# A two-layer transformer trunk: the compressed branch's inputs laid out token by token, by engines in place of four transfers

## The chip, the cores and the metric

The kernel runs on one core of a Trainium2 chip. The metric is device time in microseconds (us), the median of several runs. Before the change it is 640.43 us (three runs, 640.12 to 640.68).

## The reference, cut to what matters

Two layers of a decoder for 256 tokens of 1024 features, in float32: `x += mixer(norm(x))` and `x += relu(norm(x) @ w1)^2 @ w2` in each, then a last norm. The first layer's mixer joins native sparse attention (compressed, selected and window branches) with differential attention; the second layer's is block attention. The change touches the compressed branch's keys and values only:

```
def compress_kv(kv, pos, w1, w2):                  # keys or values: 2 heads (g) of 64
    nc = (s - CMP_BLOCK) // CMP_STRIDE + 1         # 15 windows of 32 tokens, one every 16
    tok = jnp.arange(nc)[:, None] * CMP_STRIDE + jnp.arange(CMP_BLOCK)[None, :]
    blk = kv[:, :, tok] + pos
    hid = jax.nn.gelu(blk.reshape(b, g, nc, CMP_BLOCK * d) @ w1)      # 2048 -> 128
    return hid @ w2                                                   # 128 -> 64
...
    lc = jnp.einsum('bgrqd,bgcd->bgrqc', qb, kc) * scale + tbl_gr[:, :, t5_bucket(rel_c)]
    pc = masked_softmax(lc, rel_c >= 0)            # the compressed branch
    oc = jnp.einsum('bgrqc,bgcd->bgrqd', pc.astype(vc.dtype), vc)
```

## The kernel before, in words

**Numbers in two parts.** Every matmul operand is split into a high part (a copy to a shorter format, ScalarE) and a low part (the rest, VectorE); a product is three matmuls: high x high, high x low, low x high (`mm3`, L530 to L532). Weights come from HBM in pieces of 128x1024 through five raw buffers (SyncE's queue, `load`, L403) and are split by ScalarE (L470) and VectorE (L473) into one of six pairs of parts.

**The stages.** Layer 0's projections go unit by unit in the order vg, k, q0, c, q1, h, dv, d0 to d3. "c" gives the inputs of the compression, "h" is its first layer (`unit_hid`, L1026). The softmax maps of the window and selected branches begin when their q unit is done; the first two query groups' maps run beside q1, h and dv. Behind h stand `cmp_hidden` (the activation and second layer), `cmp_softmax` (the compressed logits of all heads), and the values. The maps of the other two query groups begin when the first two have given back their two banks of PSUM, which takes the compressed branch's values as well. The differential heads and the output projection follow.

**The first layer of the compression.** `got_ckv` (L926) takes the bank of unit c, 128 rows (two heads of 64 features) by 2 x 256 (keys and values, tokens), writes a high copy (ScalarE, L515) and a low part (VectorE, L521) to a tile `kcv`, and lays both out in `mT[1]` (named mTl in the trace, not yet in use for the mixer's output). There the lower 64 partitions hold the first half of a window's tokens and the upper 64 the second half. The layout is by part, key or value, head, block (15, and a sixteenth that holds the positional terms), and the 16 tokens of a half innermost. Four transfers on SyncE's queue bring `kcv` there, one for each head and half. The first layer then runs 16 steps of two matmuls (L1039 and L1040: weights high and low, 256 columns), each with one token's 128 values (part, key or value, head, block) as the stationary operand, so neighbours of this operand lie 16 elements apart.

**What sets the order.** No engine is scheduled by hand. A planner (`Plan`, L201) runs a rough model of the engines: each step has a duration, an urgency (lower goes first) and the events it waits for, and each engine takes the most urgent step that is ready. The steps are issued in that order, and each engine's queue runs them in that order on the chip. Steps of `got_ckv` have urgency 0; a map's steps 0.001 times its number; units of columns 1; a weight split -1 if its piece is among the next two in use, else 3. A map's scaling (L827) can be done by GpSimd or VectorE, whichever is free first in the model. A bank of PSUM is read by one engine at a time: a step on another engine waits in the model for 0.2 us behind the last reader.

Of the kernel before, what the change touches and what calls it, by code (L numbers as in the profile page):

```python
# [177 lines left out]
def t_dve(n):  # L178
    return 0.0685 + n / 960
# [21 lines left out]
class Plan:  # L201
    """Puts the program's steps out in the order in which a rough model of the engines begins them:
    each engine takes the most urgent step whose inputs are there."""
# [17 lines left out]
    def when(self, deps, line, fn):  # L221
        """Calls fn as soon as the line can see all of deps done."""
        deps = [d for d in deps if d is not None]
        left = [sum(d.time is None for d in deps)]

        def go():
            t = max([self.now] + [d.time + (0.0 if d.line in (line, None) else SEEN) for d in deps])
            self.at(t, fn)

        def one():  # L230
            left[0] -= 1
            if not left[0]:
                go()

        if not left[0]:
            go()
        else:
            for d in deps:
                if d.time is None:
                    d.then.append(one)  # L240

    def step(self, choices, deps=(), urgency=1, bank=None):
        """choices: (line, time, emit) of the engines that can do the step."""
        self.count += 1
        s = Step(urgency, self.count, bank)
        for line, dur, emit in choices:
            self.when(deps, line, lambda line=line, dur=dur, emit=emit: self.arrive(line, s, dur, emit))
        return s.done
# [44 lines left out]
    def spawn(self, gen):  # L293
        """Runs gen; each value it yields is the events it waits for."""
        ev = Event()

        def go():
            try:
                w = next(gen)
            except StopIteration:  # L300
                self.fire(ev)
                return
            w = [w] if isinstance(w, Event) else w
            self.when(w, None, go)

        self.at(self.now, go)
        return ev
# [8 lines left out]
class Slots:  # L316
    """Buffers that are handed on; the one who gets it waits for its last use."""
# [22 lines left out]
    def recall(self, item):  # L340
        """Takes an item out as soon as it is free."""
        ev = Event()
        if any(item is i for i in self.items):
            self.items = [i for i in self.items if i is not item]
            self.plan.fire(ev)
        else:
            self.wanted.append((item, ev))
        return ev
# [14 lines left out]
@with_exitstack  # L363
def trunk_kernel(ctx: ExitStack, tc: tile.TileContext, x, w, prm_d, gs, cst_d, eye, out, widths):
# [32 lines left out]
    def load(dst, src, deps=(), line=SP, u=0, lat=1.3):  # L397
        """A transfer: issued by an engine, then in turn with the others on the queues."""
        eng = {SP: nc.sync, ACT: nc.scalar, POOL: nc.gpsimd}[line]
        n = int(np.prod(dst.shape)) * 4  # L400
        ev = Event()
        dur = {SP: 0.45, ACT: 0.4, POOL: 1.04}[line]
        issued = plan.step([(line, dur, lambda: eng.dma_start(dst, src))], deps, u)  # L403

        def move():
            Plan.moved = max(Plan.moved, plan.now + lat) + n / 0.34e6
            plan.at(Plan.moved + 0.5, lambda: plan.fire(ev))

        plan.when([issued], None, move)
        return ev  # L410
# [4 lines left out]
    def halves(pair):  # L415
        """Room for two pieces in a pair of tiles that are not in use."""
        v = [a.rearrange("p k s -> p (k s)") for a in pair]
        return [(v[0][:, 1024 * i:1024 * i + 1024], v[1][:, 1024 * i:1024 * i + 1024]) for i in range(2)]
# [92 lines left out]
    def split_out(hi, lo, src, n, deps, scale=None, bank=None, u=0):  # L511
        """The high part by ACT, the rest by DVE."""
        def high():
            if scale is None:
                nc.scalar.activation(hi, src, AF.Copy)  # L515
            else:
                nc.scalar.activation(hi, src, AF.Copy, scale=scale)

        def low():
            if scale is None:  # L520
                nc.vector.tensor_tensor(lo, src, hi.bitcast(F32), OP.subtract)  # L521
            else:
                nc.vector.scalar_tensor_tensor(lo, src, scale, hi.bitcast(F32), op0=OP.mult, op1=OP.subtract)  # L523

        e = act(t_act(n), high, *deps, u=u, bank=bank)
        return [e, dve(t_dve(n), low, e, u=u, bank=bank)]
# [7 lines left out]
    def rstd(t, deps):  # L534
        """(mean(x[t]^2) + eps)^-1/2; ACT squares the left columns and DVE the right ones, starting from the left's
        sum where those come first."""
# [22 lines left out]
    def rvar(t, deps):  # L559
        """1 / (mean(x[t]^2) + eps)."""  # L560
# [6 lines left out]
    def to_xT(t, g, xT, xe, rs, deps, back=()):  # L567
        """Steps that write x[t] * g (* rs) transposed into xT."""
# [78 lines left out]
    def unit_N(src, cuts, n, done):  # L647
        """One bank of columns for each row tile."""
# [13 lines left out]
    def units_N(src, dones):  # L662
        """Two banks of columns for each row tile; part of the second comes before the second tile's first."""
# [16 lines left out]
    def row_mm(bank, src, deps, pc, kt, t, n, prev, first, last, u=1):  # L680
        """bank += rows t of src's column tile kt @ half n of the piece's columns."""
# [57 lines left out]
    begun = []  # L739

    def urgency():
        """Earlier maps go first."""
        begun.append(0)
        return 0.001 * len(begun)

    def logits_exp(q, k, par, h, P, sums, b, deps, u):
        """exp(q.k + bias - max) of one map: [q0 x k0 | q1 x k0 k1], and the row sums."""
# [30 lines left out]
    def turned_P(A, deps, u):  # L778
        """The transposed probabilities, in two parts."""
# [24 lines left out]
    def head_map(q, k, par, h, v, v_e, gate, pair, deps, seen=None):  # L804
        """One causal softmax map of a head; its part of the pair's outputs is added to po."""
# [32 lines left out]
    class Pair:  # L838
        """The outputs of two heads, gathered in one bank."""
# [27 lines left out]
    # ================= layer 0: mixer =================  # L867
# [26 lines left out]
    def first_norms():  # L894
        """g over all rows by the tensor engine; it stays in PSUM for the time."""
# [27 lines left out]
    ckv = mT[1].rearrange("p (h k g) (c i) -> p h k g c i", h=2, k=2, c=16)  # L923
    ckv_e = Event()

    def got_ckv(b, evs):  # L926
        """Both parts of the compression's inputs, the second half-block's tokens below the first's."""
        kcv = acts.tile([128, 2, 2, S], F32R, name="kcv", tag="scr")
        ps = b.t.rearrange("p (a t) -> p a t", a=2)
        ev = split_out(kcv[:, 0], kcv[:, 1], ps, 512, evs, bank=b)  # L930
        bank_a.put(b, [ev[1]])
        pos = prm[:, P_POS:P_POS + 32].rearrange("p (k i) -> p k i", k=2)[:, :, None, :].to_broadcast([128, 2, 2, 16])
        done = split_out(ckv[:, 0, :, :, 15, :], ckv[:, 1, :, :, 15, :], pos, 64, [prm_e])
        for g in range(2):
            for s in range(2):
                done.append(load(ckv[64 * s:64 * s + 64, :, :, g, 0:15, :].rearrange("p h k c i -> p (h k) (c i)").bitcast(F32),
                                 kcv[64 * g:64 * g + 64, :, :, 16 * s:16 * s + 240].rearrange("p h k t -> p (h k) t").bitcast(F32),
                                 ev))
        yield done
        plan.fire(ckv_e)  # L940

    def stack_q(dst, ps, b, deps, u=0):
        """Both parts of q / 8 of a head's rows: one in the head's half, the other in the other half."""
# [11 lines left out]
    def stack_k(hi, lo, ps, b, deps, u=0):  # L955
        """The high part of k twice, and the low part over zeros."""
# [69 lines left out]
    def unit_hid():  # L1026
# [5 lines left out]
        for q in range(4):  # L1032
            pc = next_piece()
            for ii in range(4):
                def emit(pc=pc, q=q, ii=ii):
                    pc.use()
                    c = slice(256 * ii, 256 * ii + 256)
                    lhs = ckv[:, :, :, :, :, 4 * q + ii]
# [10 lines left out]
    def cmp_hidden(ba, e):  # L1049
        """Compressed keys and values."""  # L1050
# [51 lines left out]
    def cmp_softmax():  # L1102
        """The compressed branch of the eight heads in one."""
# [176 lines left out]
    def add_to_x(bank, slots, dep, t, n, rs=None):  # L1280
        """x[t] += bank (* rs)."""
# [11 lines left out]
    def out_proj(m_e, x_free, nxt):  # L1293
        """x += m @ w; the first tokens go ahead, and their norm runs beside the products of the others.
        Two of the pieces lie in the room of the transposed x."""
# [38 lines left out]
    def mlp(src, x_ready, nxt):  # L1334
        """x += relu(norm(x) @ w1)^2 @ w2, the norm's factor of each token squared at the end."""
# [21 lines left out]
        def turned(t, b, evs):  # L1357
            """Tokens are the rows here: to be turned."""
# [76 lines left out]
    def next_stage(gi, norm):  # L1435
        """The transposed (normed) x of the next stage, one token tile after the other."""
# [19 lines left out]
    def program():  # L1456
# [19 lines left out]
        # layer 1  # L1476
# [44 lines left out]
    def final(t, evs):  # L1521
# [4 lines left out]
        def job():  # L1526
            """x * g waits for the norm's factor."""
# [40 lines left out]
```

## Time and profile before

| | |
|---|---|
| median of the runs | 640.43 us (640.12 to 640.68) |
| profiled execution, span from its first to its last instruction | 638.6 us (the page gives no other time of it) |
| busy: TensorE, weight loads | 623.5 us, 562.5 us |
| busy: VectorE, ScalarE, GpSimd | 402.3, 358.8, 80.8 us |
| granted clock of TensorE, mean | 0.996 |
| moved by DMA | 110.49 MB, 173 GB/s |

Instructions of TensorE are pipelined, and the profile shows each with its whole length, so their lengths add up to more than the time; what one costs is the distance from its start to the next one's start. Weight loads have a row of their own (PEld) and overlap the matmuls. A wait in the profile is the idle time of an engine ahead of an instruction, put down to what released it last. Names: `ps` is a bank of PSUM, `whi` and `wlo` a weight piece's parts, `xTh` and `xTl` the transposed tokens' parts, `P` a map, `mTl` the tile in which the compression's inputs lie.

### The profile page before, as it was taken

The page shows a single profiled execution, that of the slowest core. Times are in us where ns is not written, and L with a number is a line of the kernel's source. Part 1 is how long each engine was busy: PE and PEld are TensorE (multiplying, and loading weights), DVE is VectorE, ACT ScalarE, POOL GpSimd, SP SyncE. Part 2 cuts the span into 40 slices and gives each one's busy share as a digit, 9 for nine tenths or more (in the row PEclk, how much of TensorE's full clock was granted, in tenths as well). Part 3 has the DMA queues.
Part 4 walks back from the last instruction along what each step waited for, and adds up shares of the span by engine and source line. Part 5 has one row for each costly group of instructions (what it writes and reads, how often), then busy time and mean ns, then how long its engine had stood idle before and what let it go on. Part 6 is the DMA issues. An engine that isn't in the chain of part 4 may idle for free.

```text
span 638.6 us, 10541 instructions
## 1 busy us (share of the span) xinstructions
PE 623.5 (98%) x4022; PEld 562.5 (88%) x4022; DVE 402.3 (63%) x723; ACT 358.8 (56%) x645; POOL 80.8 (13%) x105
## 2 busy tenths in 40 slices
PE   7999999999999999999999999999999999999995
PEld 5999899778899898999988999978889999898994
DVE  6888698869554545445477688785964454544434
ACT  6777488747645445444444588764764444445421
POOL 2022022210201001011120020110020100101011
PEclk8999999999999999999999999999999999999999
DMA  7995432325765565656527433443576555565501
GB/s 280 320 304 190 141 105 96 131 101 185 256 212 191 179 199 165 204 191 214 183 73 236 155 121 111 132 133 120 173 267 202 195 179 193 176 200 176 165 2 66
DMA packets 33188, 110.49 MB, mean 173 GB/s; under 512 B 3425, under 2 KB 6769, under 8 KB 33138
## 3 DMA queue, kind: packets, MB, share of 16 engines
q1 hardware_dynamic: 32274, 107.21, 51.7%
q0 software_dynamic: 576, 2.10, 0.9%
q8 instruction: 31, 0.51, 0.3%
q10 hardware_dynamic: 288, 0.52, 0.2%
q14 instruction: 19, 0.16, 0.1%
HBM read 107.76 MB, written 1.07 MB: 170 GB/s over the span
## 4 chain that ended last, share of the span: by engine, by line
PE 86%; DVE 6%; ACT 4%; issue 2%; DMA 1%; POOL 1%; SPq 0%; POOLq 0%; DVEq 0%; ACTq 0%
PE ps L531 26%; PE ps L530 26%; PE ps L532 26%; PE ps L756 2%; DVE wlo L473 2%; PE ps L790 1%; DVE KZ L964 1%; PE ps L593 1%; DVE QD L951 1%; ACT KD L961 1%; DMA x<-in_x_dram 1%; ACT QD L947 1%; POOL P L827 1%; ACT KD L960 1%; PE ps L1040 1%
## 5 line engine op out<-in xcount | busy, mean ns | idle before, releaser
L473 DVE TENSOR_TENSOR wlo<-raw,whi 128x1024 fp32r<-128x1024 f32 (+1 forms) x157 | 189.3, 1217 | 74.1 <-ACT whi L470 72.6
L470 ACT ACTIVATE whi<-raw 128x1024 fp32r<-128x1024 f32 (+1 forms) x157 | 163.5, 1052 | 96.8 <-PE ps L532 70.3
L530 PE MATMUL ps<-xTh,whi 128*128 128x256 f32 x592 | 168.9, 285 | 0.0
L531 PE MATMUL ps<-xTl,whi 128*128 128x256 f32 x592 | 166.4, 281 | 0.0
L532 PE MATMUL ps<-xTh,wlo 128*128 128x256 f32 x592 | 166.3, 281 | 0.0
L530 PEld LDWEIGHTS ps<-xTh,whi 128*128 128x128 f32 x592 | 111.7, 189 | 1.1 <-ACT gates L996 0.3
L531 PEld LDWEIGHTS ps<-xTl,whi 128*128 128x128 f32 x592 | 111.7, 189 | 0.7
L532 PEld LDWEIGHTS ps<-xTh,wlo 128*128 128x128 f32 x592 | 111.6, 189 | 0.0
L1348 POOL TENSOR_TENSOR P<-P 128x512 f32<-128x512 f32 x32 | 35.8, 1120 | 320.5 <-ACT P L1345 319.0
L473 DVE TENSOR_TENSOR mTl<-raw,mTh 128x1024 fp32r<-128x1024 f32 x34 | 43.2, 1272 | 23.9 <-ACT mTh L470 23.9
L470 ACT ACTIVATE mTh<-raw 128x1024 fp32r<-128x1024 f32 x34 | 36.0, 1059 | 30.2 <-PE ps L531 20.4
L1345 ACT ACTIVATE P<-ps 128x512 f32<-128x512 f32 x32 | 19.0, 595 | 52.2 <-PE ps L532 52.2
L530 PE MATMUL ps<-whi,Th 128*128 128x512 f32 x120 | 46.9, 391 | 0.0
L532 PE MATMUL ps<-whi,Tl 128*128 128x512 f32 x120 | 46.9, 391 | 0.0
L531 PE MATMUL ps<-wlo,Th 128*128 128x512 f32 x120 | 46.9, 390 | 0.0
L1350 DVE TENSOR_TENSOR Tl<-P,Th 128x512 fp32r<-128x512 f32 x22 | 15.2, 693 | 50.1 <-POOL P L1348 50.1
L770 ACT ACTIVATE P<-P,nm 128x128 f32<-128x128 f32 x80 | 35.5, 447 | 13.5 <-DVE nm L766 13.5
L532 PE MATMUL ps<-xTh,mTl 128*128 128x256 f32 (+1 forms) x128 | 38.1, 297 | 0.7 <-DVE mTl L523 0.7
L530 PE MATMUL ps<-xTh,mTh 128*128 128x256 f32 (+1 forms) x128 | 38.7, 302 | 0.0
L531 PE MATMUL ps<-xTl,mTh 128*128 128x256 f32 (+1 forms) x128 | 38.0, 297 | 0.0
L530 PE MATMUL ps<-whi,xTh 128*128 128x512 f32 (+1 forms) x88 | 34.2, 389 | 0.0
L531 PE MATMUL ps<-wlo,xTh 128*128 128x512 f32 (+1 forms) x88 | 33.3, 378 | 0.2 <-DVE wlo L473 0.2
(219 smaller groups left out, 1193.0 us busy)
## 6 DMA issues: line engine op xcount, KB each, us to landing
raw<-in_w_dram SPq DMA_DIRECT2D x192, 512.0 KB, 4.1
B<-ud SPq DMA_DIRECT2D x1, 2048.0 KB, 11.3
gB<-in_gs_dram POOLq DMA_DIRECT2D x4, 512.0 KB, 4.3
x<-in_x_dram SPq DMA_DIRECT2D x2, 512.0 KB, 4.4
mTl<-kcv SPq DMA_DIRECT2D x4, 240.0 KB, 6.8
raw<-in_w_dram SPq DMA_DIRECT2D x2, 420.0 KB, 6.2
out_dram<-P SPq DMA_DIRECT2D x2, 256.0 KB, 2.0
out_dram<-P ACTq DMA_DIRECT2D x2, 256.0 KB, 2.5
```

The costliest lines, as they stand in the source:

```text
L470: nc.scalar.activation(pc.hi[:, :n], raw[:, :n], AF.Copy)
L473: nc.vector.tensor_tensor(pc.lo[:, :n], raw[:, :n], pc.hi[:, :n].bitcast(F32), OP.subtract)
L530: nc.tensor.matmul(out_, ah, bh, start=start, stop=False)
L531: nc.tensor.matmul(out_, ah, bl, start=False, stop=False)
L532: nc.tensor.matmul(out_, al, bh, start=False, stop=stop)
L593: nc.tensor.transpose(p[:, 128 * k:128 * k + 128], xs[:, 128 * k:128 * k + 128], ident)
L756: nc.tensor.matmul(ps[:, 128 * qt:128 * qt + nk], q[:, par, ts], k[i][:, par, :nk], start=i == 0, stop=i == 1)
L770: nc.scalar.activation(P[:, c], P[:, c], AF.Exp, bias=nm[:, qt:qt + 1], scale=-1.0, accum_out=sums[:, qt:qt + 1])
L790: nc.tensor.transpose(pt[:, c], A[:, c], ident)
L1345: e = act(t_act(512), lambda: nc.scalar.activation(r, b.t, AF.Relu), got, *deps)
L1348: g = pool(1.225, lambda: nc.gpsimd.tensor_tensor(sq, r, r, OP.mult), e)
L1350: h = dve(t_dve(512), lambda: nc.vector.tensor_tensor(hl, sq, hh.bitcast(F32), OP.subtract), f, g)
```

## The change: a new layout, and engine copies for the four transfers

The inputs lie by token first and block last: `ckv_rows[:, i]` is the 128 values of token i, side by side, and is the stationary operand of step i. `kcv` holds the high copy alone (one ScalarE copy of the whole bank, 128x512). For each of the four pairs of head `g` and half `s`, the 64 partitions of the head go to the 64 partitions of the half: the high part by GpSimd from `kcv` where both are the same partitions, else by ScalarE from the bank; the low part by VectorE, from the bank and `kcv`. Each of these handles 64 partitions x 480 elements, reads at a distance of 16 elements and writes runs of 15. The positional terms are written at every sixteenth element. The bank goes back when all readers of it are done. The comments of the file are taken out as well.

```diff
-    ckv = mT[1].rearrange("p (h k g) (c i) -> p h k g c i", h=2, k=2, c=16)
+    ckv_rows = mT[1].rearrange("p a b -> p (a b)").rearrange("p (i m) -> p i m", i=16)
+    ckv = ckv_rows.rearrange("p i (h k g c) -> p h k g i c", h=2, k=2, g=2)
...
-        kcv = acts.tile([128, 2, 2, S], F32R, name="kcv", tag="scr")
+        kcv = acts.tile([128, 2, S], F32R, name="kcv", tag="scr")
         ps = b.t.rearrange("p (a t) -> p a t", a=2)
-        ev = split_out(kcv[:, 0], kcv[:, 1], ps, 512, evs, bank=b)
-        bank_a.put(b, [ev[1]])
+        whole = act(t_act(512), lambda: nc.scalar.activation(kcv, ps, AF.Copy), *evs, bank=b)
...
-        done = split_out(ckv[:, 0, :, :, 15, :], ckv[:, 1, :, :, 15, :], pos, 64, [prm_e])
+        done = split_out(ckv[:, 0, :, :, :, 15], ckv[:, 1, :, :, :, 15], pos, 64, [prm_e])
+        out = []
         for g in range(2):
+            r = slice(64 * g, 64 * g + 64)
             for s in range(2):
-                done.append(load(ckv[64 * s:64 * s + 64, :, :, g, 0:15, :].rearrange("p h k c i -> p (h k) (c i)").bitcast(F32),
-                                 kcv[64 * g:64 * g + 64, :, :, 16 * s:16 * s + 240].rearrange("p h k t -> p (h k) t").bitcast(F32),
-                                 ev))
+                o, t = slice(64 * s, 64 * s + 64), slice(16 * s, 16 * s + 240)
+                def part(h, src, r=r, o=o, t=t, g=g):
+                    return ckv[o, h, :, g, :, 0:15], src[r, :, t].rearrange("p k (c i) -> p k i c", i=16)
+                def hi(part=part):
+                    dst, src = part(0, ps)
+                    nc.scalar.activation(dst, src, AF.Copy)
+                def same(part=part):
+                    dst, src = part(0, kcv)
+                    nc.gpsimd.tensor_copy(dst, src.bitcast(F32))
+                def lo(part=part):
+                    (dst, src), (_, high) = part(1, ps), part(1, kcv)
+                    nc.vector.tensor_tensor(dst, src, high.bitcast(F32), OP.subtract)
+                if g == s:
+                    done.append(pool(0.9, same, whole))
+                else:
+                    out.append(act(t_act(480), hi, *evs, bank=b))
+                out.append(dve(t_dve(480), lo, whole, bank=b))
+        bank_a.put(b, [whole, *out])
+        done += out
         yield done
...
-                    lhs = ckv[:, :, :, :, :, 4 * q + ii]
+                    lhs = ckv_rows[:, 4 * q + ii]
```

## Rows read from the trace of the kernel before

**Rows 1.** The page, part 1: busy us (share of the span) and instructions per engine.

```profile
PE 623.5 (98%) x4022; PEld 562.5 (88%) x4022; DVE 402.3 (63%) x723; ACT 358.8 (56%) x645; POOL 80.8 (13%) x105
```

**Rows 2.** The page, part 4: shares of the chain that ended last, by engine.

```profile
PE 86%; DVE 6%; ACT 4%; issue 2%; DMA 1%; POOL 1%; SPq 0%; POOLq 0%; DVEq 0%; ACTq 0%
```

**Rows 3.** Stretches: length, busy us of each engine (instructions), granted clock, DMA share, GB/s.

```profile
37.50:61.40 23.90, 23.90 (x177) 23.77 (x176) 20.76 (x66) 19.43 (x52) 7.24 (x9) 1.00 0.70 214
61.40:73.70 12.30, 12.30 (x70) 10.55 (x69) 6.81 (x14) 3.99 (x7) 0.14 (x2) 1.00 0.40 124
73.70:105.00 31.30, 31.30 (x254) 30.45 (x254) 29.33 (x97) 24.24 (x70) 6.24 (x7) 1.00 0.43 138
105.00:129.00 24.00, 22.32 (x156) 19.69 (x154) 21.18 (x65) 19.36 (x59) 4.88 (x8) 1.00 0.33 117
```

**Rows 4.** Instructions on tile mTl up to 150 us: duration ns min/median/max, first and last start.

```profile
L1039 PEld LDWEIGHTS ps<-whi,mTl x16: 291/316/318, 49.6 to 58.3; 128*128 128x128 f32 x16
...
L403 SPq DMA_DIRECT2D mTl<-kcv x4: 600/692/1673, 40.0 to 42.1; - x4
...
DMA to landing us min/median/max: 6.6/6.8/7.2
```

**Rows 5.** The page, part 5: a projection's weight loads, busy us and mean ns of one.

```profile
L531 PEld LDWEIGHTS ps<-xTl,whi 128*128 128x128 f32 x592 | 111.7, 189 | 0.7
```

**Rows 6.** The chain that ended last from 49.5 to 59 us, by line.

```profile
by line: PE ps L1040 37.6%; PE ps L1039 37.5%; PE ps L790 10.6%; PE ps L530 6.6%; PE ps L532 4.9%; PE ps L531 4.8%; PE ps L756 1.3%
```

**Rows 7.** Timeline of TensorE: start us, length us, engine, line, operation, out<-in.

```profile
36.32 0.28 PE L530 MATMUL ps<-xTh,whi 128*128 128x256 f32 x1
...
39.44 0.28 PE L532 MATMUL ps<-xTh,wlo 128*128 128x256 f32 x1
...
49.61 0.48 PE L1039 MATMUL ps<-whi,mTl 128*128 128x256 f32 x1
```

**Rows 8.** Timeline of SyncE's queue from 40 us.

```profile
40.03 3.79 SPq L403 DMA_DIRECT2D mTl<-kcv  x4
```

**Rows 9.** TensorE's waits (20 to 160 us; then weight loads, whole span): total us, times, longest.

```profile
PE ps L530 <- DVE KZ L964: 1.1, 1, 1.1
...
PEld ps L790 <- POOL P L827: 1.8, 4, 0.7
```

**Rows 10.** Instructions on tile kcv.

```profile
L515 ACT ACTIVATE kcv<-ps x1: 597/597/597, 38.7 to 38.7; 128x512 fp32r<-128x512 f32 x1
L521 DVE TENSOR_TENSOR kcv<-ps,kcv x1: 690/690/690, 39.3 to 39.3; 128x512 fp32r<-128x512 f32 x1
```

**Rows 11.** Groups on ScalarE, then VectorE, 30 to 60 us: busy us, mean ns of one.

```profile
L947 ACT ACTIVATE G<-ps 64x256 fp32r<-64x256 f32 x8 | 3.0, 378 | 0.6 <-PE ps L532 0.5
...
L964 DVE TENSOR_TENSOR KL<-ps,KK 64x256 fp32r<-64x256 f32 x1 | 0.4, 427 | 0.0
```

**Rows 12.** The compressed logits' additions, by source line: duration ns min/median/max.

```profile
L1133 DVE TENSOR_TENSOR cmpb<-ps,B x4: 192/222/254, 73.8 to 74.4; 128x28 f32<-128x28 f32 x2, 128x60 f32<-128x60 f32 x2
...
L1140 DVE TENSOR_TENSOR cmpb<-cmpb,ps x2: 215/247/279, 74.1 to 74.7; 128x56 f32<-128x56 f32 x1, 128x120 f32<-128x120 f32 x1
```

**Rows 13.** Timeline of VectorE: the splits of weights between 34 and 60 us.

```profile
34.67 2.36 DVE L473 TENSOR_TENSOR wlo<-raw,whi 128x1024 fp32r<-128x1024 f32 x2
...
45.73 1.22 DVE L473 TENSOR_TENSOR wlo<-raw,whi 128x1024 fp32r<-128x1024 f32 x1
...
58.31 2.35 DVE L473 TENSOR_TENSOR wlo<-raw,whi 128x1024 fp32r<-128x1024 f32 x2
```

**Rows 14.** Timelines of GpSimd and of the weight loads: the first map's scaling and transposes.

```profile
40.55 0.61 POOL L827 TENSOR_SCALAR P<-P,co,gates 128x256 f32<-128x256 f32 x1 [31.45 <-DVE co L820]
...
42.05 0.35 PEld L790 LDWEIGHTS ps<-ident,P 128*128 128x128 f32 x3
```

**Rows 15.** GpSimd's scalings: by source line, then the longest in the timeline.

```profile
L827 POOL TENSOR_SCALAR P<-P,co,gates x15: 449/626/2746, 40.5 to 99.7; 128x256 f32<-128x256 f32 x14, 128x128 f32<-128x128 f32 x1
...
58.21 2.71 POOL L827 TENSOR_SCALAR P<-P,co,gates 128x256 f32<-128x256 f32 x1 [4.56 <-DVE co L820]
```

## The prediction

> **What bounds the kernel now.** I read the busy table first: TensorE is busy for 98% of the span, VectorE for 63% and ScalarE for 56% [rows 1]. The chain of work that ended last says the same, 86% of the span on TensorE [rows 2]. The whole kernel is then a queue of matmuls, and whatever shortens a matmul pays unless an engine that feeds it is late. So the stage around the change is read by stretches [rows 3]: from 37.5 to 105 us TensorE has no gap, and its granted clock is 1.00, the 2.4 GHz level. VectorE is busy for 20.76 of 23.90 us up to 61.4, for only 6.81 of 12.30 us after it, and for 29.33 of 31.30 us up to 105. Only from 105 to 129 us does TensorE lose time (22.32 of 24.00).
>
> In this stage the 32 matmuls of the compression's first layer stand out. Their weight loads take 316 ns [rows 4], while every projection's load of the same 128x128 takes 189 [rows 5]. They are the instructions that read the compression's inputs with 16 elements between neighbours. From 49.5 to 59 us the chain is theirs for 37.6 + 37.5% of 9.5 us [rows 6], which is 7.13 us, or 0.223 us for each. A projection also streams 256 columns per matmul and starts one every 0.12 us: its 27 starts from 36.32 to 39.44 us span 26 intervals [rows 7]. The moving columns are equal, so I put the difference down to the weight load.
>
> **The change part by part.**
>
> *The layout.* The 128 weights of each matmul now lie side by side, as in a projection. Both operands then have the projection's form, so I take its interval: 32 x (0.223 - 0.120) = 3.30 us less on TensorE, on the path. Bounds: 0 if the distance is not the reason, 3.4 if the interval comes down to 0.117.
>
> *The transfers removed.* Four issues on SyncE took 3.79 us from 40.03 us, and each landed 6.8 us after its issue [rows 4, 8]; the last, issued at 42.1, landed at about 48.9. TensorE came to the first layer at 49.6 and did not wait for them: its longest wait between 20 and 160 us is 1.1 us, for a later stage [rows 7, 9]. Nothing on the path goes with them. The issues and the traffic are worth 0; what is gained is that the inputs can be ready earlier, and no one needs them earlier than 49.6 less what TensorE gains on the way. Bounds: 0 to -0.3.
>
> *ScalarE.* The whole-bank copy stays: before 597 ns for 128x512 [rows 10]. Added are two copies of 64x480. By the nearest rows, 378 ns for 64x256 [rows 11] and 597 for 128x512, one takes about 0.57, 1.1 us together. Their reads step over 16 elements; if that costs what it costs the weight load (316/189 = 1.67), 1.9 us. ScalarE was busy for 19.43 of 23.90 us [rows 3], so it has 4.5 us of room and I cost it at 0.
>
> *VectorE.* One subtraction of 128x512 (690 ns) becomes four of 64x480. By the rows for 64x256 (427 ns) and 128x512 each takes 0.66, together 2.65, so 1.96 us are added. These read both operands at a distance of 16. The bias addition of the compressed logits reads one operand so: from 28 to 60 elements it grows from 192 to 254 ns, 1.94 ns per element, where a packed one grows from 215 to 279 ns between 56 and 120 elements, 1.0 ns [rows 12]. At 1.94 one takes 0.14 + 480 x 0.00194 = 1.07, together 4.3, so 3.6 us are added. I lean to the upper half, some 3 us, since the row with the same distance is the nearer one. In the stretch from 37.5 to 61.4 VectorE had 3.14 us without work, and TensorE now wants to leave this stretch 3.3 us earlier, so up to 3 us of VectorE's work no longer fits. What can move is there: two weight splits (2.35 us) stand at 58.31 [rows 13], for pieces that TensorE comes to only after some 65 us, and the 12.3 us behind 61.4 have 5.5 us of room [rows 3]. So the sum of the work costs 0 on the path; its place does not.
>
> *Its place.* The four subtractions and the copies come at about 39.3 to 44 us, at a higher urgency than the first softmax maps, whose VectorE and GpSimd steps run there. The first map's scaling on GpSimd ran from 40.55 to 41.16 and its transposes on TensorE began at 42.05 [rows 14], so there was 0.9 us to spare. Behind the waiting transpose stands all of TensorE, and nothing else can pass it. The plan that lays out the order counts 0.57 us for a subtraction and 0.9 us for a GpSimd copy, and puts q's columns ahead of the transposes accordingly; only what the operations take beyond that can stall TensorE. For VectorE that is 4 x (1.07 - 0.57) = 2.0 us at the upper price and 0.4 at the lower, less the 0.9 to spare: a stall of 0 to 1.1 us. I take 0.6.
>
> *GpSimd.* Two copies of 64x480 from SBUF. The rows for scaling 256 and 128 elements, 626 ns (the median) and 449 (the shortest, the one with 128) [rows 15], give 1.38 ns per element, so 0.93 us each. The longest of these rows took 2746 ns: it ran from 58.21 while VectorE did two splits [rows 13, 15], whose two inputs both lie in SBUF. Two such copies would end 5.4 us after 39.3 instead of 1.9. No split stood on VectorE between 37.0 and 45.7 [rows 13], so I take 0.93 each, inside the plan's 0.9, and 0 on the path.
>
> The Trainium skill speaks against this part. GPSIMD Engine Reference, section Performance pitfalls for Q7 kernels, says that a read of SBUF with more than 8 bytes between elements costs some half more per element; these copies step 64 bytes. By it a copy would take about 1.3 us, an estimate from that page, and the sum would come to 638.4 if all of the 0.7 us beyond two copies of 0.93 became waiting; no row of this case shows it.
>
> *Small ones.* The positional part is written at single elements instead of runs of 16; 242 and 219 ns at 30 us, far ahead of its use. The bank of the inputs is held some 3 us longer; the next user of that pair comes at 49.6. Both 0.
>
> Sum: -3.30 + 0.6 = -2.7 us. The path behind this stage is TensorE's to 105 us and then follows the last projection through ScalarE and VectorE, so I carry it to the end in full. The profiled execution has a span of 638.6 us, and the median of the three runs is 640.43, so 1.8 us lie around the span, which the change does not touch. 640.43 - 2.7 = 637.7.
>
> **The rivals.**
>
> *A, the engines take it back.* TensorE gains 3.3 us but VectorE, at 94% from 73.7 to 105 us, does not: it would have to start that stretch earlier, and the compressed logits that start it come through a chain of small VectorE steps that stand behind the extra 3 us. For it: the 94%. Against it: VectorE's 5.5 us of room just ahead, and TensorE's lack of waits [rows 9]. If all but 0.5 to 1 us is lost: 639.4 to 640; with the 3 us of VectorE work fully on the path, 640.1.
>
> *B, slower: the first maps starve TensorE.* One mechanism: the two GpSimd copies stand ahead of the first four scalings in GpSimd's queue, and a weight split on VectorE beside them stretches each to 2.7 us. Then the first scaling ends at 39.3 + 5.4 + 0.6 = 45.3 instead of 41.2, and TensorE, which reaches the transposes at 42 us plus what the plan puts ahead of them, stands still for up to 4 us, and for another 0.9 with the subtractions at their upper price. It decides the sign from a stall of 3.3 us on; at 4.9 it gives 642.0. For it: TensorE has already waited for these scalings, 1.8 us in four places of the whole span [rows 9]. Against it: no split stood there.
>
> *C, more than the term.* The inputs are ready earlier, the compressed branch ends earlier, and the maps of the last four query groups start earlier, which fills part of the 1.7 us that TensorE loses after 105: 635.5.
>
> *D, it doesn't do what it says.* The 316 ns are not due to the distance. Then only the stall of 0.6 us is left: 641.0. Against it: no other difference to a projection's load is to be seen.
>
> **How the numbers follow.** Forecast (636.4 to 639.1): 0.60. A: 0.18, of which 0.04 below 639.1, 0.12 within 0.2% and 0.02 above. B: 0.10. C: 0.07. D: 0.05, of which 0.01 is slower. A measurement of this kernel tells about 0.2%, 1.3 us, from no change: faster is below 639.1, slower above 641.7. Faster: 0.60 + 0.07 + 0.04 = 0.71. Same: 0.12 + 0.04 = 0.16. Slower: 0.10 + 0.02 + 0.01 = 0.13. The range from 635.9 to 640.9 leaves out most of C's lower part (0.05) and B with the worst of A and D (0.13).
>
> **What would show it.** Right: weight loads of the first layer at 189 ns, a start every 0.12 us, its 32 matmuls in 3.8 us, four subtractions of 0.66 to 1.07 us, TensorE's waits for scalings near 41 to 46 us below 1 us in sum, the same share of TensorE after 129 us. Wrong: loads that stay at 316 (D); GpSimd copies above 2 us with transposes waiting for scalings (B); a first layer 3.3 us shorter with waits of TensorE for VectorE between 61 and 129 us (A).

## The result, and the profile after

The changed kernel takes 647.36 us (median of four runs, 646.16 to 648.28; the kernel before beside it 640.55). The ratio is 1.0099, interval 1.0085 to 1.0113: it is slower by some 6.3 us, where 2.7 us less were forecast. Below, a difference in us is a run's ratio less one, times 640.5; the intervals of such ratios are 0.1 to 0.25% to either side.

The first layer itself did what was forecast. The rows on tile mTl of the changed kernel (duration in ns, least, median, most; first and last start) answer to [rows 4, 10]:

```profile
L1063 PEld LDWEIGHTS ps<-whi,mTl x16: 187/188/190, 45.6 to 50.6; 128*128 128x128 f32 x16
...
L954 DVE TENSOR_TENSOR mTl<-ps,kcv x4: 992/998/1007, 40.4 to 43.4; 64x480 fp32r<-64x480 f32 x4
...
L946 ACT ACTIVATE mTl<-ps x2: 564/568/571, 39.2 to 39.8; 64x480 fp32r<-64x480 f32 x2
L950 POOL CAST mTl<-kcv x2: 1018/1026/1035, 39.2 to 40.3; 64x480 fp32r<-64x480 f32 x2
```

The timeline of TensorE has 26 matmuls of the layer in a row:

```profile
47.89 0.29 PE L1063 MATMUL ps<-whi,mTl 128*128 128x256 f32 x1
...
50.82 0.28 PE L1064 MATMUL ps<-wlo,mTl 128*128 128x256 f32 x1
```

The loads fell from 316 to 188 ns, and these 25 intervals are 0.117 us each, where 0.223 was before and 0.120 was forecast. The layer's last matmul starts at 50.8 us instead of 58.6. The page's busy times and its chain, which answer to [rows 1, 2], tell that TensorE bounds less of the time than before (75% of the chain for 86%) and VectorE more (12% for 6%):

```profile
PE 627.1 (97%) x4022; PEld 561.8 (87%) x4022; DVE 405.5 (63%) x727; ACT 360.5 (56%) x647; POOL 78.4 (12%) x106
...
PE 75%; DVE 12%; ACT 5%; DMA 3%; issue 3%; POOL 1%; SPq 0%; POOLq 0%; DVEq 0%; ACTq 0%
```

The stretches of the changed kernel, with the columns of [rows 3], show what came of it:

```profile
37.50:61.40 23.90, 22.09 (x164) 20.14 (x163) 22.48 (x67) 19.01 (x51) 4.67 (x8) 1.00 0.54 192
61.40:73.70 12.30, 12.30 (x80) 10.81 (x79) 10.69 (x27) 6.17 (x13) 1.24 (x2) 1.00 0.39 129
73.70:105.00 31.30, 30.66 (x250) 29.70 (x250) 27.69 (x94) 23.74 (x70) 5.28 (x9) 1.00 0.31 102
105.00:129.00 24.00, 22.14 (x155) 19.90 (x154) 20.10 (x54) 17.80 (x48) 4.57 (x7) 1.00 0.41 130
129.00:144.00 15.00, 15.00 (x82) 12.70 (x81) 7.04 (x24) 7.37 (x22) 2.28 (x5) 1.00 0.19 74
144.00:164.00 20.00, 16.24 (x66) 12.18 (x65) 15.91 (x24) 10.34 (x16) 0.00 (x0) 0.83 0.64 210
```

TensorE, the first busy time, was without a gap in the first stretch before; now 1.81 us are missing there. The large loss is far from the change, in the last stretch, which before read:

```profile
144.00:164.00 20.00, 20.00 (x112) 17.01 (x111) 17.01 (x23) 15.24 (x21) 1.35 (x1) 1.00 0.68 222
```

The same 20 us now hold 66 matmuls for 112. The timeline of TensorE in the changed kernel shows the place, from the transposes of the last differential head's outputs (L1290) and the output projection's last product (148.60) over the transposes of the normed tokens (L593) to the first turn of the next part (L1400):

```profile
144.32 0.38 PE L1290 MATMUL ps<-ident,od 128*128 128x128 f32 x2
...
148.60 0.40 PE L532 MATMUL ps<-whi,mTl 128*128 128x512 f32 x1
149.99 0.66 PE L593 MATMUL ps<-ident,P 128*128 128x128 f32 x4 [0.99 <-DVE P L577]
151.32 0.65 PE L593 MATMUL ps<-ident,P 128*128 128x128 f32 x4 [0.67 <-DVE P L577]
153.12 1.11 PE L593 MATMUL ps<-ident,P 128*128 128x128 f32 x4 [1.14 <-DVE P L577]
153.88 0.78 PE L530 MATMUL ps<-whi,xTh 128*128 128x512 f32 x1
154.46 0.63 PE L531 MATMUL ps<-wlo,xTh 128*128 128x512 f32 x1
...
163.75 0.60 PE L1400 MATMUL ps<-ident,P 128*128 128x128 f32 x4
```

The kernel before, the same places (L1266 and L1376 are L1290 and L1400 now), with the first tile's transposes (L593) and the first product of the MLP (147.78):

```profile
138.31 0.38 PE L1266 MATMUL ps<-ident,od 128*128 128x128 f32 x2
...
143.42 0.60 PE L593 MATMUL ps<-ident,P 128*128 128x128 f32 x4
...
147.54 0.40 PE L532 MATMUL ps<-whi,mTl 128*128 128x512 f32 x1
147.78 0.39 PE L530 MATMUL ps<-whi,xTh 128*128 128x512 f32 x1
...
155.65 0.60 PE L1376 MATMUL ps<-ident,P 128*128 128x128 f32 x4
```

Before, the first token tile had been normed while the output projection still ran, so its MLP products began 0.24 us behind it. Now both tiles' norms come after it, VectorE works through them without a pause, and TensorE has nothing else. The new order brings the last differential head later, its outputs' transposes at 144.32 us instead of 138.31, and the output projection has to wait for them with its last part. Up to there little was lost: counted in the trace, the matmul behind the first 950 starts at 143.87 us, before at 143.19, and the one behind the first 1000 at 160.95, before at 152.85. After the stops at 149 to 153 us the granted clock is near the 1.2 GHz level for some 5 us (the third number from the end; the third busy time is VectorE's):

```profile
152.00:156.00 4.00, 2.88 (x9) 2.50 (x10) 3.97 (x8) 3.96 (x7) 0.00 (x0) 0.52 0.22 86
156.00:160.00 4.00, 4.00 (x14) 3.21 (x14) 3.88 (x7) 0.85 (x2) 0.00 (x0) 0.63 0.56 164
```

So 8.11 us from 147.54 to 155.65 became 15.15 from 148.60 to 163.75. The output projection ended 1.06 us later than before, these 7.04 come on top (part of them the first tile's transposes, which stood ahead of it before), and everything behind is shifted by the 8.1.

### The profile page after: what moved, and what is told of

It reads as the page before. It is cut to its first block, busy times and chain, and to the rows that moved or that the text cites. A ratio compares the mean times of both kernels' runs of the same rounds, so it can differ in the third digit from the quotient of the medians.

```text
span 646.5 us, 10538 instructions
## 1 busy us (share of the span) xinstructions
PE 627.1 (97%) x4022; PEld 561.8 (87%) x4022; DVE 405.5 (63%) x727; ACT 360.5 (56%) x647; POOL 78.4 (12%) x106
## 3 DMA queue, kind: packets, MB, share of 16 engines
HBM read 107.76 MB, written 1.07 MB: 168 GB/s over the span
## 4 chain that ended last, share of the span: by engine, by line
PE 75%; DVE 12%; ACT 5%; DMA 3%; issue 3%; POOL 1%; SPq 0%; POOLq 0%; DVEq 0%; ACTq 0%
PE ps L531 24%; PE ps L530 24%; PE ps L532 24%; DVE wlo L473 3%; DMA B<-ud 2%; PE ps L756 1%; DVE Tl L521 1%; ACT KD L985 1%; DVE KZ L988 1%; PE ps L790 1%; DVE QD L975 1%; ACT KD L984 1%; PE ps L593 1%; ACT QD L971 1%; DVE P L766 1%
```

## The experiments

Two suspects were clear from these views: the copies in front of the first maps (theory I), and the new order, since a planner that is told of other steps puts the whole program out in another order (theory II). "Old order" below means that the planner was shown the steps of before, and that the queues of TensorE, VectorE, ScalarE and GpSimd are those of before but for the steps named. In the expectations theory II is called O at first, and O+P adds the copies' place; in those of the old kernel reading side by side and of the copies on GpSimd, I stands for the layout's gain being real. The diffs show the lines that matter of each kernel; their comments point to the others.

### Change without new order, new order without change

**The change's instructions in the old order.** The copies are put out inside the planner's old steps:

```diff
+        def high():   # in the old step of ScalarE; low() in VectorE's: the four subtractions
+            nc.scalar.activation(kcv, ps, AF.Copy)
+            for g in range(2):
+                nc.scalar.activation(*part(g, 1 - g, 0, ps), AF.Copy)
+                dst, src = part(g, g, 0, kcv)
+                nc.gpsimd.tensor_copy(dst, src.bitcast(F32))
```

> The changed kernel's layout and engine copies, issued in the order of the kernel before (the planner is shown the old steps and transfers, so every other instruction keeps its place). Theory O (the new order of the queues costs the time, the copies themselves little): the first layer's matmuls gain 3.3 us, the longer VectorE block costs up to 2.5 us in waits near 42 to 46 us, so 637 to 640 us. Theory I (the copies themselves cost it: 4 us of VectorE ahead of the first maps starve TensorE, and the clock falls behind that): 644 us or more in any order.

Measured: 644.28 us, ratio 1.0062 (1.0045 to 1.0079), +4.0 us. VectorE's and then TensorE's timeline, and two stretches:

```profile
40.38 3.91 DVE L946 TENSOR_TENSOR mTl<-ps,kcv 64x480 fp32r<-64x480 f32 x4 [2.17 <-ACT mTl L938]
```

```profile
41.92 0.28 PE L532 MATMUL ps<-xTh,wlo 128*128 128x256 f32 x1
45.46 0.56 PE L790 MATMUL ps<-ident,P 128*128 128x128 f32 x3 [3.26 <-DVE nm L766]
```

```profile
46.00:48.00 2.00, 2.00 (x13) 2.00 (x12) 1.93 (x12) 1.95 (x9) 1.47 (x3) 0.59 0.00 0
48.00:50.00 2.00, 2.00 (x13) 2.00 (x12) 1.76 (x7) 2.00 (x6) 0.73 (x2) 0.56 0.00 0
```

VectorE stands for 2.17 us, since its first subtraction waits for ScalarE's two copies, then subtracts for 3.91; the maps' steps stand behind. TensorE stops for 3.26 us, and after it runs 4 us at little over half its clock, which costs another 1.7 (4 us at a mean of 0.575). That alone is more than the layer gains.

**The order of after with the instructions of before** (transfers and one subtraction, issued at the places of the copies), **and the old instructions with the planner told another time for one step** (the planner gives one scaling to GpSimd instead of VectorE; the rest is order):

```diff
-                prev = pe(0.22, emit, prev, pc.ready, ckv_e, u=1)
+                prev = pe(0.446, emit, prev, pc.ready, ckv_e, u=1)
```

> The reverse: the order of the changed kernel, with the instructions of the kernel before (two ScalarE and VectorE passes, four transfers, stationary operand at a distance of 16). Theory O: the order carries its loss with it, and the first layer is 3.3 us slower again: 647 to 651 us, with waits of TensorE for VectorE from 144 to 158 us. Theory I: without the copies the loss is gone: 640 to 643 us.

> The kernel before, instruction for instruction; only the planner is told that a pair of the first layer's matmuls takes 0.446 us, as the trace has it, instead of 0.22. Nothing but the order changes. Theory O: the time moves by more than 1 us, either way, up to several us. Theory I: 640 to 641 us, as before.

Measured: 654.75 us, 1.0220 (1.0205 to 1.0236), and 648.02, 1.0105 (1.0082 to 1.0127). In the first, 4.6 us are one wait for the transfers, which this order wants sooner, and the waits for L577 at the end of the layer are there again, 2.5 us. The second has the work of before, in another order, and is 6.7 us slower, with waits in other places:

```profile
PE ps L1266 <- DVE od L1256: 1.4, 1, 1.4
PE ps L531 <- DVE xTl L473: 0.9, 1, 0.9
```

**The changed kernel with the planner told what the copies take** (1.05, 1.01 and 0.58 us), **and with the copies at an urgency behind the maps**:

```diff
-                    done.append(pool(0.9, same, whole))
+                    done.append(pool(1.05, same, whole))       # the first kernel
+                    done.append(pool(0.9, same, whole, u=0.5)) # the second
```

> The changed kernel with one difference: the planner is told what the copies take in the trace (VectorE 1.01 us instead of 0.57, GpSimd 1.05 instead of 0.9, ScalarE 0.58 instead of 0.45), so the order differs again. If the loss is the planner's wrong idea of these times, 637 to 642 us. Theory O in its plain form (any shift in these steps gives another order, good or bad): somewhere from 637 to 650 us, not tied to the better numbers. Theory I: 645 to 649 us, as the instructions are the same.

> The changed kernel with one difference: the planner gives the copies urgency 0.5, so that the first maps' steps go first. The order differs again from all others. Theory O+P: the stops at 44 to 46 us go, but the order behind is drawn anew, so 637 to 648 us, not tied to the smaller cost; a time below 640 would be luck of the order. If the place ahead of the first maps were the only loss in the changed kernel: 638 to 641 us.

Measured: 646.74 us, 1.0093 (1.0076 to 1.0110), and 648.91, 1.0115 (1.0092 to 1.0138). Neither is telling the planner the truth nor moving the copies back a cure. The first has no waits at the layer's end but loses as much elsewhere, 2.3 us of it in one wait behind the compression's first layer; the second has all of them (L593 for L577: 2.8 us).

**The changed kernel without its copies**, in its own order (`mTl` is set to zero once, far ahead, so the compression's inputs are missing):

```diff
                 def lo(part=part):
-                    (dst, src), (_, high) = part(1, ps), part(1, kcv)
-                    nc.vector.tensor_tensor(dst, src, high.bitcast(F32), OP.subtract)
+                    pass          # hi and same likewise
```

> The changed kernel in its own order, with the eight copies and subtractions of 64x480 left out (the tile is set to zero far ahead, so the compression's inputs are left out). Theory II (the new order of the rest of the program costs most of the loss): 643 to 646 us, the last differential head as late as in the changed kernel, and TensorE's waits for VectorE at 144 to 158 us still there. Rival (the copies themselves, in front of the first maps, cost the loss): 636.5 to 639 us, with no such waits.

Measured: 644.86 us, 1.0072 (1.0057 to 1.0087), +4.6 us. Its waits, its first and its last stretch, and the two marks at the layer's end:

```profile
PE ps L593 <- DVE P L577: 2.8, 3, 1.1
...
37.50:61.40 23.90, 23.90 (x179) 22.20 (x177) 20.82 (x68) 18.90 (x53) 2.65 (x6) 1.00 0.57 196
...
144.00:164.00 20.00, 16.98 (x74) 13.38 (x75) 15.43 (x24) 10.52 (x15) 0.00 (x0) 0.91 0.53 185
```

```profile
146.40 0.39 PE L532 MATMUL ps<-whi,mTl 128*128 128x512 f32 x1
...
160.30 0.60 PE L1398 MATMUL ps<-ident,P 128*128 128x128 f32 x4
```

With the copies gone, the gaps of the first stretch are gone, and the last products of the differential values' unit start 3.2 us earlier than before (71.55 for 74.79 us). Six matmuls fewer stand ahead of them in this order, so by the number of matmuls the lead is about 2 us. Then the last differential head's logits come at 129.1 instead of 123.3, and the norms stand uncovered at the layer's end: the output projection's last product is still 1.1 us earlier than before (146.40 for 147.54), and the next part begins 4.7 us later (160.30 for 155.65). That is the order's doing alone.

### What the layout is worth in the old order

**The old kernel, reading 128 neighbours** (the values it multiplies are in the wrong order):

```diff
-                    lhs = ckv[:, :, :, :, :, 4 * q + ii]
+                    lhs = mT[1].rearrange("p a b -> p (a b)")[:, 128 * (4 * q + ii):128 * (4 * q + ii) + 128]
```

> The kernel before with one edit: the matmuls of the compression's first layer read 128 neighbouring elements of the inputs' tile, so the values they read are in the wrong order; transfers, engine steps and the order of all queues are those of before. Theory I (the layout's 3.3 us is real and reaches the end wherever the order and the feeding engines stay as they were): weight loads at 189 ns, the first layer some 3.3 us shorter, 637.0 to 637.8 us. Rival (VectorE, 94% busy behind this stage, takes the gain back; or the transfers land too late for an earlier layer): 639.2 us or more, with new waits of TensorE for VectorE between 61 and 129 us.

Measured: 639.41 us, 0.9986 (0.9974 to 0.9997): only 0.9 us of 3.3. The loads are at 188 ns. What stops TensorE now, in its waits, GpSimd's timeline and TensorE's:

```profile
PE ps L790 <- POOL P L827: 1.1, 1, 1.1
...
PE ps L1039 <- DMA mTl<-kcv: 0.5, 1, 0.5
```

```profile
56.87 2.72 POOL L827 TENSOR_SCALAR P<-P,co,gates 128x256 f32<-128x256 f32 x1 [3.60 <-ACT cmpb L1056]
```

```profile
58.23 0.31 PE L790 MATMUL ps<-ident,P 128*128 128x128 f32 x1
59.64 0.44 PE L790 MATMUL ps<-ident,P 128*128 128x128 f32 x2 [1.11 <-POOL P L827]
```

The first is the scaling of [rows 15], 2.7 us long beside two splits. Before, it ended at 60.92 and its transposes came at 61.26; TensorE, now 3 us earlier, arrives ahead of its end. The second is no work of the edit, which changes nothing ahead of the first layer: in this execution the transfers took 8.1 to 8.7 us to land, before 6.6 to 7.2 [rows 4], and the next kernel's trace does not have the wait. The two come to 1.6 of the 2.4 us that are missing.

**That scaling on VectorE**, in this kernel, and in the kernel before as a control:

```diff
+        return nc.vector if len(scaled) == 8 else nc.gpsimd
```

> The old kernel reading 128 neighbouring elements (values in the wrong order, as before), and its eighth scaling of a map by GpSimd (2.7 us long beside two weight splits) done by VectorE ahead of these splits. Theory: the wait of 1.1 us goes, the wait of 0.5 us for the transfers stays: 638.0 to 638.8 us. Rival (the splits are late by the scaling's 0.4 us and the piece is missed, or the gain is lost further on anyway): 639.4 us or more.

> The kernel before with that eighth scaling on VectorE alone. Theory: TensorE did not wait for it there (it ended 0.3 us ahead of its transposes), so no difference: 640.2 to 640.8 us. Rival (the move gains or costs something of its own): beyond 0.6 us either way.

Measured: 638.39 us, 0.9962 (0.9947 to 0.9976), 2.4 us less; the control 640.83, 0.9999 (0.9989 to 1.0008). The move is worth nothing by itself and gives back 1.5 us here; no wait for a scaling is left. Most of the 3.3 us does reach the end, then, in the old order, with this one scaling moved and nothing added.

### The copies' place and engine, in the old order

**Four subtractions behind the maps' first steps, ScalarE's and GpSimd's copies later:**

```diff
+                late.append(dve(0.0, lambda g=g, s=s: low(g, s), wait(1.5 + 2.0 * g + 1.0 * s), u=0.5))
```

> The order of the kernel before, as in e1, with the new layout and all the engine copies, but the four subtractions stand one by one behind the first maps' steps on VectorE, and ScalarE's and GpSimd's copies behind the first maps' exponentials and scalings. Theory O+P (the gain of 3.3 us in the first layer is real; it is lost by the copies' place ahead of the first maps, and in the changed kernel by the new order on top): TensorE no longer stops at 42 us, the clock stays, 637 to 639 us. Theory I (the copies' work itself costs the time wherever it stands, since VectorE is at 87% and more): 641 to 644 us.

Measured: 643.60 us, 1.0038 (1.0024 to 1.0052). The first stop is gone, but not the work: the subtractions now stand between the maps' transposed parts, and the clock falls again.

```profile
PE ps L531 <- DVE Tl L521: 2.2, 2, 1.6
```

```profile
50.00:52.00 2.00, 2.00 (x11) 2.00 (x10) 1.93 (x4) 1.98 (x6) 0.18 (x1) 0.50 0.00 0
```

**Packed reads, scattered writes** (the old-order kernel, neighbours read side by side and written 128 elements apart):

```diff
-            return ckv[o, h, :, g, :, 0:15], src[r, :, t].rearrange("p k (c i) -> p k i c", i=16)
+            return ckv[o, h, :, g, :, 0:15].rearrange("p k i c -> p k c i"), src[r, :, t].rearrange("p k (c i) -> p k c i", i=16)
```

> As e1 (old order, copies ahead of the first maps), but each copy reads packed elements and writes them at a distance of 128, instead of reading at a distance of 16 and writing runs of 15. If the reads' distance is what makes a subtraction take 1.0 us, it takes 0.65 now, VectorE's block shrinks from 3.9 to 2.6 us and TensorE's stop from 3.3 to about 2: 641 to 643 us. If the distance costs the same on the writing side, or the two inputs set it: 1.0 us and 644 us again.

Measured: 645.56 us, 1.0073 (1.0058 to 1.0089).

```profile
L946 DVE TENSOR_TENSOR mTl<-ps,kcv x4: 955/964/1014, 41.4 to 44.3; 64x480 fp32r<-64x480 f32 x4
L938 ACT ACTIVATE mTl<-ps x2: 1015/1025/1035, 39.3 to 40.3; 64x480 fp32r<-64x480 f32 x2
```

TensorE's stop ahead of the maps' transposes is longer, 4.2 us instead of 3.26. VectorE takes about 1 us whichever side is scattered; ScalarE takes 0.57 with scattered reads and 1.03 with scattered writes.

**VectorE left as it was** (one packed subtraction); ScalarE's two copies stay, GpSimd makes the other six between its scalings; and all eight on GpSimd:

```diff
+            late.append(pool(0.0, lambda c=c: copy(*c), wait(TIMES[n]), u=0.5))
```

> The order of before, the new layout, no transfers; the low parts are made by one packed 128x512 subtraction as before, ScalarE makes the two high copies that cross partitions right behind its whole copy, and GpSimd makes the other six copies of 64x480 (1.03 us each) between its scalings. Theory I, and that the loss of the old-order kernels came from VectorE's 3 us in front of the first maps: no stop of TensorE above 1.5 us between 38 and 62 us, 637.5 to 639.5 us, faster than both. Rival (any engine's copies at this place starve TensorE, GpSimd's by delaying the scalings): stops of 2 us or more behind L827, a clock below 0.9, 642 us or more.

> As the kernel before this one, with all eight copies on GpSimd and none added on ScalarE. 8 x 1.03 us of copies beside 6 scalings of 0.63 us want 12 us, from 39.3 to 51.3; the layer wanted its inputs at 49.6. Theory I: scalings 0.5 to 1 us late, the first layer 1 to 2 us late but 3.3 us shorter, 638 to 640 us. Rival (starving): 642 us or more, and worse than with the two copies on ScalarE.

Measured: 641.71 us, 1.0015 (1.0006 to 1.0025), and 641.95, 1.0023 (1.0012 to 1.0033). Better than any other home of the copies so far, and missed by 2 us. In the first, VectorE still stood for 2.17 us:

```profile
40.84 0.69 DVE L948 TENSOR_TENSOR kcv<-ps,kcv 128x512 fp32r<-128x512 f32 x1 [2.17 <-ACT mTl L936]
```

In the second the first layer waited 1.5 us for GpSimd, whose copies took up to 2.97 us for two beside VectorE's splits instead of 2.1.

**Mended**: ScalarE's two copies behind the third exponential, so that VectorE need not wait for them; the six on GpSimd one at a time; the long scaling on VectorE.

```diff
+            late.append(act(0.0, lambda g=g: cross(g), wait(0.0), u=-1))
```

> The order of before, the new layout, no transfers; one packed subtraction on VectorE as before; the two high copies that cross partitions on ScalarE behind the third exponential, so that VectorE does not wait for them; six copies on GpSimd, one between two scalings; the eighth scaling on VectorE. Theory: VectorE's 2.2 us without work at 38.7 and the 1.3 us wait for the scaling go: 638.8 to 640.0 us, faster than the kernel before by 0.1 to 0.25%. Rival (GpSimd's copies and the 1.15 us more on ScalarE starve TensorE whatever their order): 641 us or more, with the first layer waiting for GpSimd's copies.

Measured: 640.61 us, 0.9997 (0.9988 to 1.0005): no different from the kernel before. VectorE's 2.17 us and TensorE's wait for the long scaling are gone as the theory has it, but the copies still cost 2.2 us (from -2.4, the layout with the scaling moved, to -0.2). The first stretch of [rows 3], where TensorE had no gap, shows 1.81 us of gaps, in pieces of 0.2 to 0.6:

```profile
37.50:61.40 23.90, 22.09 (x178) 21.00 (x177) 21.99 (x65) 20.84 (x55) 12.13 (x15) 1.00 0.44 154
```

ScalarE is fuller than before (20.84 for 19.43), and VectorE and GpSimd slow each other. VectorE's timeline, then GpSimd's:

```profile
41.84 0.35 DVE L833 TENSOR_SCALAR P<-P,co,gates 128x128 f32<-128x128 f32 x1
...
42.85 0.82 DVE L833 TENSOR_SCALAR P<-P,co,gates 128x128 f32<-128x128 f32 x1
...
44.12 1.18 DVE L833 TENSOR_SCALAR P<-P,co,gates 128x128 f32<-128x128 f32 x1
...
47.30 1.79 DVE L473 TENSOR_TENSOR wlo<-raw,whi 128x1024 fp32r<-128x1024 f32 x1
```

```profile
42.56 1.01 POOL L946 CAST mTl<-kcv 64x480 fp32r<-64x480 f32 x1
...
44.17 1.03 POOL L946 CAST mTl<-kcv 64x480 fp32r<-64x480 f32 x1
...
45.92 2.09 POOL L946 CAST mTl<-kcv 64x480 fp32r<-64x480 f32 x2
```

A scaling of 0.35 us takes 0.82 and 1.18 where a copy of GpSimd overlaps it, and a split beside GpSimd's work 1.79 instead of 1.22. How the 2.2 us divide between this and the fuller ScalarE was not tested. No kernel was found that does the whole change and is faster than the one before.

## Why the prediction was wrong

The parts, from the kernels that have one of them: the layout read for nothing in the old order, -0.9 us; the new order, +5.5 (from -0.9 to +4.6); the copies in that order, +1.7 (from +4.6 to +6.3), which agrees with the 1.81 us of gaps in the first stretch that the kernel without copies does not have. The parts depend on the path. With the copies already in the old order (+4.0) the new order adds 2.3 more, and with the old transfers it costs 14.1.

- *The layout*, -3.30: right on TensorE (188 ns, a start every 0.117 us, which by 32 matmuls is 3.4 us; the first layer's end comes 7.8 us earlier, part of it by order).
- *Carried to the end in full*: wrong, and the costliest step, for two reasons. The forecast treated the order of all work behind this stage as unchanged. The planner derives that order from the steps' durations and engines; four transfers were replaced by eight engine steps, so the order had to change, and its price was never asked. It is 5.5 us beside the layout alone, and it was paid at 144 to 164 us, where the profile of before showed no trouble. Even where the order stays, only 0.9 us arrived: a scaling with 0.3 us to spare became a wait of 1.1 us. Its row was read [rows 15], for GpSimd's price alone; I asked what the changed steps delay, not what is just in time for a TensorE that comes 3 us sooner.
- *Its place*, 0.6: mis-sized. The term was the subtractions' excess over what the planner counts. In the old order it is 4.9 us (from -0.9 to +4.0): the stop of 3.26 and the 1.7 that the low clock costs behind it. The kernel's other long stop, 1.3 us for the long scaling, is there without copies too (1.1). In the new order, which does put q's columns ahead as I had assumed, 1.7. Left out were VectorE's wait for ScalarE's two copies and the clock after a stop.
- *VectorE*, 4 x 1.07 leaned to: 1.00 measured, right. *ScalarE*, 0.57: right, but not hidden, for VectorE stands behind it (0.7 us in the changed kernel, 2.17 in the old order). *GpSimd*, 0.93: 1.03 measured, 2.11 for both, and unstretched. The Trainium skill's rule (GPSIMD Engine Reference, Performance pitfalls for Q7 kernels) would have made it 1.3, an estimate from that page; the runs lie between, nearer to the forecast.
- *Transfers*, 0: right in the old order, though with less room than it had read: by the longest landing of [rows 4], 7.2 us, the last was there at 49.3, just ahead of TensorE at 49.6; with the old instructions in the new order, where the layer comes sooner, TensorE waited 4.6 us for them.
- *Rival B*, the slower one, had the right sign (0.10), but the first maps are the place of the smaller part only, the copies' 1.7 us, and the engine is the wrong one: VectorE's queue starved them, not a stretched GpSimd. No rival named the place of the larger part. *Rival A*'s loss between 61 and 129 us is 0.8 us more than before (TensorE is busy for 30.66 and 22.14 us in the last two of these stretches, before 31.30 and 22.32), short of the 2.3 that A needed.

That the order of before is an unusually good one is what four others suggest: the new one without the copies (+4.6 us), the two retold planners' (+6.0 and +7.4, copies and all), and one with no other edit (+6.7). Why a planner's order is worse was followed to its waits in the changed kernel's own alone; what in the model's step times leads to it stays open.

## What to carry to other kernels

Where a planner or scheduler sets the order, a local edit reorders the whole program: price that by running the old instructions in the new order and the new instructions in the old one, before anything is said of the edit. Where TensorE gains time, list what becomes ready just ahead of it downstream: a slack of 0.3 us took 1.5 of a gain of 3.3 here. And work moved from a transfer queue to engines that stand between TensorE and its next operands can cost more than its busy time: here TensorE stopped for 3.26 us and then ran at little over half its clock for 4 more.

## What the runs showed of the hardware

- After TensorE stopped for 3.26 us (41.92 to 45.46) its granted clock was 0.59 and 0.56 in the following 46 to 50 us, and 1.00 from 50 on; after a series of stops of 0.7 to 1.1 us at 149 to 153 it was 0.52 and 0.63 up to 160. Matmuls of 512 columns take 0.63 us there instead of 0.40. A single stop of 1.11 us (to 59.64, in the old kernel reading side by side) was followed by 1.00.
- A weight load of 128x128 takes 316 ns with 16 elements between neighbours and 188 with neighbours side by side, and matmuls of 256 columns behind it start every 0.223 and every 0.117 us.
- VectorE takes about as long for a 64x480 subtraction with elements 16 apart on the side read (1.00 us) as with them 128 apart on the side written (0.96). ScalarE's copy of 64x480 takes 0.57 us with scattered reads and 1.03 with scattered writes, and the estimate for packed elements, from [rows 10, 11], is 0.57 too.
- VectorE and GpSimd slow each other both ways: GpSimd's scaling goes from 0.6 to 2.7 us and its two copies from 2.1 to 2.97 beside VectorE's splits, VectorE's scaling from 0.35 to 1.18 beside GpSimd's copies.
